# First layer: the low parts of the input weights made on GpSimd instead of VectorE

## The chip, the cores and the metric

One program on one core of a Trainium2 chip. The time is device microseconds of one execution. The kernel before took 3749.44 us as the median of three runs (3739.95 to 3749.61).

## The reference, cut to what matters

Two layers are applied to a prompt of 2048 frames and to 32 sample frames, all in float32. The first layer, the only one whose code changes, is

```
h = rms_norm(x, g) * (1 + scale) + shift            # 2048 x 1024
q, k, v, z = split(h @ w_in, 4)                     # w_in is 1024 x 4096
q, k = rms_norm(q), rms_norm(k)                     # per head of 64, 16 heads
o = attend(q, k, v, bias by clipped distance, chunks of 64, a band of 8 earlier chunks)
x = x + gate * (o * silu(z)) @ w_out
```

The second layer is latent attention with the same frame around it.

## The kernel before, in words

Every float32 matrix product is made of three TensorE products: each operand is held as a high part (rounded to the matmul's format) and a low part (the operand minus its high part). `mm3` (line 187, its products are lines 189, 190 and 191) adds high by high, high by low and low by high into one PSUM bank.

The first layer runs through 32 steps (the list `steps`): two halves of the prompt, in each half eight groups of two heads, and for each group two blocks of 512 frames. A step does the attention of its group and block (`prep`, `scores`, `values`, `finish`), and beside it, piece by piece by a plan of fractions of the step, the projection of the next step (`project` for q, k and v, `project_z` for z). So a group's weights are used for two steps, and a pair of steps takes about 83 us in the first half.

The weights of the next group are brought while the second block of the current group is projected. `fetch_w` loads a chunk of 256 rows (two k tiles) into one of two raw buffers `wr`; `split_w` then writes, for each k tile, the high part on ScalarE (line 458) and the low part on VectorE (line 459) into one of eight `wq` tiles of 128x384. Right after the split the raw buffer is loaded again. `fetch_z` and `split_z` (lines 470 and 471) do the same for z, 128x512 in one instruction, two tiles `wz` for each group. That is eight `wq` and two `wz` low parts for each pair of steps, 16 times in the kernel: once at the start, before anything is projected, and 15 times inside the steps.

Before the attention of a step can begin, q and k get their norm: line 511 copies the projection to `raw`, line 514 squares it, line 515 sums on VectorE, `rstd` (lines 174 to 184) makes 1/sqrt in small steps on VectorE and ScalarE, and line 520 multiplies: head 0 on VectorE, head 1 on GpSimd. TensorE then transposes `raw` (line 591). GpSimd also adds up the exponentials for the softmax sums (line 678, into `acc`), makes low parts of v (line 600), and in the second half low parts for the condition vectors' projection (line 149).

Each engine works through its queue in order. The order inside a queue is not the program's: a planner of the build places the instructions by the cost that it expects, so an instruction may stand far from its neighbours in the code. The DMAs all go through the queue of SyncE, in order too.

Of the kernel before, what the change touches and what calls it, by code (L numbers as in the profile page):

```python
# [11 lines left out]
ALU = mybir.AluOpType  # L12
# [19 lines left out]
def f32(ap):  # L32
    return ap if ap.dtype == F32 else ap.bitcast(F32)
# [66 lines left out]
def trunk(ctx: ExitStack, tc: tile.TileContext, I, O, stop=99):  # L100
    nc = tc.nc
    V, S, G, T = nc.vector, nc.scalar, nc.gpsimd, nc.tensor
# [268 lines left out]
    def at1(shape, name, dt=F32, bufs=1):  # L371
        return at.tile(shape, dt, tag=name, name=name, bufs=bufs)
# [79 lines left out]
    def split_w(g, c):  # L452
        raw = raws.pop((g, c))
        for i in range(2):
            w = at1([128, 2, 384], "wq", F32R, 8)
            hi, lo = (w[:, a, :].rearrange("p (h s d) -> p s h d", h=2, s=3) for a in range(2))
            src = raw[:, 384 * i:384 * i + 384].rearrange("p (s h d) -> p s h d", s=3, h=2)
            S.copy(hi, src)
            V.tensor_tensor(lo, src, f32(hi), ALU.subtract)
            Wg[g, 2 * c + i] = w  # L460

    def fetch_z(g, c):
# [4 lines left out]
    def split_z(g, c):  # L467
        raw = raws.pop((g, "z", c))[:, 0:512].rearrange("p (i c) -> p i c", i=4)
        w = at1([128, 4, 2, 128], "wz", F32R, 2)
        S.copy(w[:, :, 0, :], raw)  # L470
        V.tensor_tensor(w[:, :, 1, :], raw, f32(w[:, :, 0, :]), ALU.subtract)
        for i in range(4):
            Wz[g, 4 * c + i] = w[:, i]

# [16 lines left out]
    def project(s):  # L491
# [5 lines left out]
        for j in range(4):  # L497
            js = slice(128 * j, 128 * j + 128)
            p = bank("mm")[:, 0:384]
            for k in range(KT):  # L500
                w = Wg[g, k]
                mm3(p, (hT[:, k, 0, js], hT[:, k, 1, js]), (w[:, 0, :], w[:, 1, :]), k == 0, k == KT - 1)
                if k % 4 == 3 and blk % 2 and s["next_g"] is not None:
                    if j == 1:
                        fetch_w(s["next_g"], k // 4)
                    elif j == 3:
                        split_w(s["next_g"], k // 4)
                        fetch_w(s["next_g"], k // 4 + 2)
                if k in (2, 5):
                    yield  # L510
            S.copy(raw[:, j, :], p)
            qk = raw[:, j, :].rearrange("p (h c) -> p h c", h=2)[:, :, 0:128]
            sq = at1([128, 4, 128], "hs").rearrange("p j t -> p (j t)")[:, 0:256]
            S.activation(sq.rearrange("p (h c) -> p h c", h=2), qk, AF.Square)
            V.tensor_reduce(s16[:, 4 * j:4 * j + 4], sq.rearrange("p (h d) -> p h d", d=64), AX.X, ALU.add)
            if j == 3:
                r = rstd(s16, 16, 1.0 / 64).rearrange("p (j h e) -> p j h e", j=4, h=2)
                for h in range(2):
                    x = raw[:, :, 192 * h:192 * h + 128].rearrange("p j (e d) -> p j e d", d=64)
                    (V, G)[h].tensor_tensor(x, x, r[:, :, h, :].unsqueeze(3).broadcast_to([128, 4, 2, 64]), ALU.mult)  # L520
            yield
# [10 lines left out]
    def project_z(s):  # L532

        g, blk = s["g"], s["blk"]
        hT = HT[blk % 2]
        p = bank("mm")
        for k in range(KT):
            z = Wz[g, k]
            mm3(p, (z[:, 0, :], z[:, 1, :]), (hT[:, k, 0, :], hT[:, k, 1, :]), k == 0, k == KT - 1)
            if k % 2:  # L540
                if k == KT - 1:
                    s["z"] = at1([128, 512], "z", bufs=2)
                    S.copy(s["z"], p)
                if blk % 2 and s["next_g"] is not None:
                    c = (k - 3) // 2
                    if k in (3, 5):
                        split_w(s["next_g"], c + 2)
                        fetch_z(s["next_g"], c)
                    elif k == 7:
                        split_z(s["next_g"], 0)  # L550
                if k == KT - 1 and blk == 0:
                    sample_rows(lambda k, n: Wz[g, k][:, n, :], 128, 3, g)
                yield
        if blk % 2 and s["next_g"] is not None:
            split_z(s["next_g"], 1)
# [184 lines left out]
    for c in range(4):  # L740
        fetch_w(0, c)
        split_w(0, c)
# [28 lines left out]
    for c in range(2):  # L771
        split_z(0, c)
# [1223 lines left out]
```

## Time and profile before

| | |
|---|---|
| median of three runs | 3749.44 us |
| profiled execution, its own time | 3754.29 us |
| its span, first to last instruction | 3752.5 us |
| TensorE busy | 3511.9 us, 94% |
| VectorE busy | 2914.7 us, 78% |
| ScalarE busy | 2173.0 us, 58% |
| GpSimd busy | 1681.1 us, 45% |
| DMA | 412.91 MB, mean 110 GB/s |

The first layer's steps lie between about 130 and 1540 us of the span; the weights of the first group are split at 44 to 58 us. In the profile's names PE is TensorE's matmuls, PEld its weight loads, DVE VectorE, ACT ScalarE, POOL GpSimd, SP SyncE. "Idle before" is the time in which an engine stood still ahead of an instruction, and the arrow says what ended it. Busy shares are means over stages with different limits, so the change is read in the stretches where the splits stand.

### The profile page before, as it was taken

The page shows a single profiled execution, that of the slowest core. Times are in us where ns is not written, and L with a number is a line of the kernel's source. Part 1 is how long each engine was busy: PE and PEld are TensorE (multiplying, and loading weights), DVE is VectorE, ACT ScalarE, POOL GpSimd, SP SyncE. Part 2 cuts the span into 40 slices and gives each one's busy share as a digit, 9 for nine tenths or more (in the row PEclk, how much of TensorE's full clock was granted, in tenths as well). Part 3 has the DMA queues.
Part 4 walks back from the last instruction along what each step waited for, and adds up shares of the span by engine and source line. Part 5 has one row for each costly group of instructions (what it writes and reads, how often), then busy time and mean ns, then how long its engine had stood idle before and what let it go on. Part 6 is the DMA issues. An engine that isn't in the chain of part 4 may idle for free. (4 is left out here: it accounts for less than half of the span.)

```text
span 3752.5 us, 57503 instructions
## 1 busy us (share of the span) xinstructions
PE 3511.9 (94%) x17834; PEld 2871.1 (77%) x17834; DVE 2914.7 (78%) x6716; ACT 2173.0 (58%) x5302; POOL 1681.1 (45%) x1744
## 2 busy tenths in 40 slices
PE   7899999989999999899989999888999999998999
PEld 4778877867777777677878888767777787777887
DVE  4788888888888888776776766788888888885653
ACT  3556555676666666542223655556776677775542
POOL 0122222344544444340012444458888888884032
PEclk9899999999999999699999999979999999999999
DMA  5222222222333333363444666563233233223253
GB/s 175 69 60 59 69 62 75 81 76 82 99 96 92 96 92 96 96 190 126 132 152 149 181 203 185 171 186 90 74 84 98 67 93 92 68 77 111 89 189 118
DMA packets 441984, 412.91 MB, mean 110 GB/s; under 512 B 68820, under 2 KB 364296, under 8 KB 434636
## 3 DMA queue, kind: packets, MB, share of 16 engines
q1 hardware_dynamic: 441676, 409.23, 37.3%
q8 instruction: 141, 2.31, 0.3%
q14 instruction: 167, 1.37, 0.1%
HBM read 251.72 MB, written 140.10 MB: 104 GB/s over the span
## 5 line engine op out<-in xcount | busy, mean ns | idle before, releaser
L1544 DVE TENSOR_REDUCE mp@325_17580<-bank 128x1 f32<-128x512 f32 (+3 forms) x384 | 233.8, 615 | 28.3 <-PE bank L1543 26.3
L675 ACT ACTIVATE bank<-bank 128x512 f32<-128x512 f32 x448 | 200.3, 447 | 0.0
L678 POOL TENSOR_TENSOR acc@61_865<-acc@61_865,P@63_893 128x256 f32<-128x256 f32 (+3 forms) x64 | 52.9, 826 | 172.4 <-ACT P@63_893 L673 143.3
L1544 DVE TENSOR_REDUCE mp@326_17581<-bank 128x1 f32<-128x512 f32 (+1 forms) x192 | 116.9, 613 | 16.7 <-PE bank L1543 16.0
L1577 ACT ACTIVATE P@436_22812<-bank 128x512 f32<-128x512 f32 (+2 forms) x156 | 83.3, 534 | 74.3 <-issue 38.6
L1577 ACT ACTIVATE P@438_22814<-bank 128x512 f32<-128x512 f32 (+2 forms) x156 | 83.2, 534 | 67.3 <-issue 35.7
L718 DVE RECIPROCAL ez@69_1265<-ez@69_1265 128x128 f32<-128x128 f32 x128 | 117.6, 926 | 0.0
L1577 ACT ACTIVATE P@437_22813<-bank 128x512 f32<-128x512 f32 (+2 forms) x156 | 83.5, 535 | 55.3 <-PE bank L1570 11.3
L1577 ACT ACTIVATE P@435_22811<-bank 128x512 f32<-128x512 f32 (+2 forms) x156 | 83.4, 535 | 54.3 <-issue 13.0
L678 POOL TENSOR_TENSOR acc@61_865<-acc@61_865,P@64_894 128x256 f32<-128x256 f32 (+3 forms) x64 | 53.2, 831 | 114.9 <-ACT P@64_894 L673 92.4
L678 POOL TENSOR_TENSOR acc@62_866<-acc@62_866,P@65_895 128x256 f32<-128x256 f32 (+3 forms) x64 | 53.9, 841 | 106.3 <-ACT P@65_895 L673 103.0
L678 POOL TENSOR_TENSOR acc@62_866<-acc@62_866,P@63_893 128x128 f32<-128x128 f32 (+3 forms) x64 | 54.1, 846 | 103.1 <-ACT P@63_893 L673 96.0
L673 ACT ACTIVATE P@64_894<-bank 128x256 f32<-128x256 f32 (+3 forms) x128 | 52.3, 409 | 76.9 <-DVE bank L667 42.1
L678 POOL TENSOR_TENSOR acc@61_865<-acc@61_865,P@65_895 128x128 f32<-128x128 f32 (+3 forms) x64 | 53.6, 838 | 95.3 <-ACT P@65_895 L673 77.5
L673 ACT ACTIVATE P@63_893<-bank 128x384 f32<-128x384 f32 (+3 forms) x128 | 52.6, 411 | 75.1 <-DVE bank L667 42.7
L673 ACT ACTIVATE P@65_895<-bank 128x128 f32<-128x128 f32 (+3 forms) x128 | 52.4, 409 | 75.0 <-DVE bank L667 44.3
L678 POOL TENSOR_TENSOR acc@62_866<-acc@62_866,P@64_894 128x256 f32<-128x256 f32 (+3 forms) x64 | 54.4, 850 | 86.9 <-ACT P@64_894 L673 84.9
L149 POOL TENSOR_TENSOR ozl@175_14851<-ozl_@180_14859,ozh@173_14849 128x1024 fp32r<-128x1024 f32 x8 | 19.3, 2412 | 151.0 <-ACT ozh@173_14849 L148 151.0
L676 DVE TENSOR_TENSOR Pl@58_862<-bank,Ph@55_859 128x512 fp32r<-128x512 f32 (+3 forms) x150 | 71.3, 475 | 18.1 <-ACT bank L675 16.4
L676 DVE TENSOR_TENSOR Pl@60_864<-bank,Ph@57_861 128x384 fp32r<-128x384 f32 (+3 forms) x149 | 71.7, 481 | 11.6 <-ACT bank L675 9.3
L676 DVE TENSOR_TENSOR Pl@59_863<-bank,Ph@56_860 128x384 fp32r<-128x384 f32 (+3 forms) x149 | 72.7, 488 | 8.3 <-ACT bank L675 5.8
L1594 DVE TENSOR_TENSOR bank<-bank,P@437_22813 128x512 f32<-128x512 f32 (+2 forms) x108 | 66.5, 616 | 12.8 <-ACT P@437_22813 L1577 12.0
(2154 smaller groups left out, 14849.6 us busy)
## 6 DMA issues: line engine op xcount, KB each, us to landing
h<-hT@203_14883 SPq DMA_DIRECT2D x16, 1024.0 KB
N<-hl@389_17976 SPq DMA_DIRECT2D x32, 512.0 KB
N<-hl@390_17977 SPq DMA_DIRECT2D x32, 512.0 KB
wr@10_296<-in_a_w_in SPq DMA_DIRECT2D x64, 192.0 KB
wr@11_297<-in_a_w_in SPq DMA_DIRECT2D x64, 192.0 KB
xr@9_231<-in_ada_w SPq DMA_DIRECT2D x32, 256.0 KB
xr@8_230<-in_ada_w SPq DMA_DIRECT2D x32, 256.0 KB
h1@220_14902<-h SPq DMA_DIRECT2D x8, 1024.0 KB
```

Source lines behind the costliest of these rows:

```text
L149: (eng or V).tensor_tensor(twin(nc, raw), raw, f32(hi), ALU.subtract)
L673: S.activation(P[:, 0:w], st[:, 0:w], AF.Exp)
L675: S.activation(st[:, 0:w], st[:, 0:w], AF.Exp)
L676: V.tensor_tensor(Pl[:, 0:w], st[:, 0:w], f32(Ph[:, 0:w]), ALU.subtract)
L678: G.tensor_tensor(u["acc"][:, qs], u["acc"][:, qs], P[:, 0:w], ALU.add)
L718: V.reciprocal(ez[:, cs], ez[:, cs])
L1544: V.tensor_reduce(mp[:, j, c:c + 1] if blk else m4[:, j:j + 1], X[:, 0:w], AX.X, ALU.max)
L1577: S.activation(P[:, 0:w], st[:, 0:w], AF.Exp)
L1594: V.tensor_tensor((u["acc"] if last else u["sum"])[:, qs], old, P[:, 0:w], ALU.add)
```

## The change

Both low parts, of `wq` and of `wz`, are subtracted by GpSimd. The high parts stay on ScalarE; the loads, buffers and program order stay as they are.

```
@@ split_w
             S.copy(hi, src)
-            V.tensor_tensor(lo, src, f32(hi), ALU.subtract)
+            G.tensor_tensor(lo, src, f32(hi), ALU.subtract)
             Wg[g, 2 * c + i] = w
@@ split_z
         S.copy(w[:, :, 0, :], raw)
-        V.tensor_tensor(w[:, :, 1, :], raw, f32(w[:, :, 0, :]), ALU.subtract)
+        G.tensor_tensor(w[:, :, 1, :], raw, f32(w[:, :, 0, :]), ALU.subtract)
```

## Rows read from the trace of the kernel before

**Rows 1.** Windows: busy us and (count) of each engine, TensorE's clock, DMA share, GB/s.
```profile
130.00:1440.00 1310.00, 1241.51 (x6450) 1016.62 (x6449) 1108.52 (x2895) 837.84 (x2104) 493.60 (x521) 0.99 0.28 80
```
**Rows 2.** Windows around the 15 splits: the third, the fourth last, the sum.
```profile
297.00:327.00 30.00, 27.16 (x141) 22.43 (x139) 26.46 (x61) 16.01 (x40) 5.92 (x7) 1.00 0.39 115
...
1203.00:1235.00 32.00, 30.38 (x143) 24.64 (x142) 26.99 (x63) 18.54 (x48) 11.91 (x13) 0.89 0.41 116
...
sum 438.00, PE 401.24 PEld 323.42 DVE 389.62 ACT 252.79 POOL 139.61; mean PE 26.75 PEld 21.56 DVE 25.98 ACT 16.85 POOL 9.31
```
**Rows 3.** Waits of TensorE, 130 to 1440 us: total us, times, longest.
```profile
PE bank L591 <- DVE raw@23_443 L520: 13.0, 15, 1.7
PE bank L659 <- DVE Pl@59_863 L676: 12.0, 18, 2.2
PE bank L659 <- DVE Pl@60_864 L676: 8.4, 17, 0.7
...
PE bank L190 <- DVE wq@16_304 L459: 2.1, 1, 2.1
```
**Rows 4.** Groups of instructions on VectorE, 44 to 1440 us: the moved instructions.
```profile
L459 DVE TENSOR_TENSOR wq@19_307<-wr@11_297,wq@19_307 128x384 fp32r<-128x384 f32 x16 | 12.4, 777 | 0.1
L471 DVE TENSOR_TENSOR wz@42_606<-wr@10_296,wz@42_606 128x512 fp32r<-128x512 f32 x16 | 12.0, 748 | 0.1
L471 DVE TENSOR_TENSOR wz@43_607<-wr@11_297,wz@43_607 128x512 fp32r<-128x512 f32 x16 | 10.9, 681 | 1.5 <-ACT wz@43_607 L470 1.4
...
L459 DVE TENSOR_TENSOR wq@16_304<-wr@10_296,wq@16_304 128x384 fp32r<-128x384 f32 x16 | 8.7, 547 | 0.0
```
**Rows 5.** Groups of instructions on GpSimd by shape, 100 to 800 us.
```profile
L436 POOL TENSOR_TENSOR HT0@0_124<-hs@20_334,HT0@0_124 128x512 fp32r<-128x512 f32 x8 | 10.7, 1335 | 27.8 <-DVE HT0@0_124 L435 27.8
...
L678 POOL TENSOR_TENSOR acc@62_866<-acc@62_866,P@65_895 128x384 f32<-128x384 f32 x9 | 10.5, 1166 | 10.2 <-ACT P@65_895 L673 7.1 <-ACT Ph@55_859 L674 2.9
...
L678 POOL TENSOR_TENSOR acc@61_865<-acc@61_865,P@64_894 128x384 f32<-128x384 f32 x8 | 8.1, 1014 | 13.5 <-ACT P@64_894 L673 13.5
```
**Rows 6.** Order on VectorE in a split window: start us, us, engine, instruction.
```profile
303.10 0.16 DVE L174 TENSOR_SCALAR ms<-s 128x16 f32<-128x16 f32 x1
...
305.64 0.17 DVE L183 SCALAR_TENSOR_TENSOR rt<-rt,ms 128x16 f32<-128x16 f32 x1
305.73 0.55 DVE L459 TENSOR_TENSOR wq@16_304<-wr@10_296,wq@16_304 128x384 fp32r<-128x384 f32 x1
306.19 0.17 DVE L184 SCALAR_TENSOR_TENSOR rs<-rt,rs 128x16 f32<-128x16 f32 x1
306.28 0.55 DVE L459 TENSOR_TENSOR wq@17_305<-wr@10_296,wq@17_305 128x384 fp32r<-128x384 f32 x1
306.75 1.54 DVE L520 TENSOR_TENSOR raw@23_443<-raw@23_443,rs 128x512 f32<-128x512 f32 x1
```
**Rows 7.** Order on GpSimd in the same window.
```profile
298.48 0.46 POOL L678 TENSOR_TENSOR acc@61_865<-acc@61_865,P@63_893 128x128 f32<-128x128 f32 x1 [7.23 <-ACT P@63_893 L673]
306.50 1.24 POOL L520 TENSOR_TENSOR raw@23_443<-raw@23_443,rs 128x512 f32<-128x512 f32 x1 [7.56 <-DVE rs L184]
```
**Rows 8.** A late window: VectorE's line 183 and the GpSimd instruction beside it.
```profile
1311.75 1.20 DVE L183 SCALAR_TENSOR_TENSOR rt<-rt,ms 128x16 f32<-128x16 f32 x1
...
1311.63 1.28 POOL L678 TENSOR_TENSOR acc@62_866<-acc@62_866,P@64_894 128x512 f32<-128x512 f32 x1 [4.51 <-ACT P@64_894 L673]
```
**Rows 9.** Durations of single lines, 130 to 1440 us: min/median/max ns, first and last start.
```profile
L183 DVE SCALAR_TENSOR_TENSOR rt<-rt,ms x37: 141/165/1202, 144.5 to 1407.1; 128x16 f32<-128x16 f32 x29, 128x1 f32<-128x1 f32 x8
L520 DVE TENSOR_TENSOR raw@23_443<-raw@23_443,rs x15: 682/1535/1693, 145.7 to 1408.4; 128x512 f32<-128x512 f32 x15
```
**Rows 10.** Order around the one wait for a split; ACT, then DVE, then PE.
```profile
834.48 0.51 ACT L458 CAST wq@16_304<-wr@10_296 128x384 fp32r<-128x384 f32 x1 [1.11 <-DMA wr@10_296<-in_a_w_in]
...
836.99 0.55 DVE L459 TENSOR_TENSOR wq@16_304<-wr@10_296,wq@16_304 128x384 fp32r<-128x384 f32 x1
837.59 0.44 PE L190 MATMUL bank<-wq@16_304,HT0@0_124 128*128 128x384 f32 x1 [2.10 <-DVE wq@16_304 L459]
```
**Rows 11.** Window of ten us after that wait, columns as in rows 1.
```profile
835.00:845.00 10.00, 6.54 (x23) 4.41 (x23) 9.69 (x19) 8.05 (x18) 4.00 (x3) 0.83 0.45 122
```
**Rows 12.** One high part on ScalarE behind its load, and its low part later on VectorE.
```profile
302.65 0.51 ACT L458 CAST wq@18_306<-wr@11_297 128x384 fp32r<-128x384 f32 x1 [0.18 <-DMA wr@11_297<-in_a_w_in]
...
313.69 0.56 DVE L459 TENSOR_TENSOR wq@18_306<-wr@11_297,wq@18_306 128x384 fp32r<-128x384 f32 x1
```
**Rows 13.** The start: first low part, last `wq` low part, first matmul, on their engines.
```profile
44.41 0.56 DVE L459 TENSOR_TENSOR wq@12_300<-wr@10_296,wq@12_300 128x384 fp32r<-128x384 f32 x1
...
51.28 0.56 DVE L459 TENSOR_TENSOR wq@19_307<-wr@11_297,wq@19_307 128x384 fp32r<-128x384 f32 x1
...
48.29 0.44 PE L189 MATMUL bank<-wq@12_300,HT0@0_124 128*128 128x384 f32 x1 [0.30 <-DVE HT0@0_124 L435]
```

More of the change, by code (lines that the diff above doesn't have):

```diff
@@ L458, in split_w @@
             S.copy(hi, src)
-            V.tensor_tensor(lo, src, f32(hi), ALU.subtract)
+            G.tensor_tensor(lo, src, f32(hi), ALU.subtract)
             Wg[g, 2 * c + i] = w
@@ L470, in split_z @@
         S.copy(w[:, :, 0, :], raw)
-        V.tensor_tensor(w[:, :, 1, :], raw, f32(w[:, :, 0, :]), ALU.subtract)
+        G.tensor_tensor(w[:, :, 1, :], raw, f32(w[:, :, 0, :]), ALU.subtract)
         for i in range(4):
```

## The prediction

> **What bounds the kernel now.** I read the busy windows of the first layer's steps first, then TensorE's waits there, then the order on VectorE and GpSimd around one split.
>
> The windows say that TensorE is the bound of this stage and VectorE is next: in 1310 us TensorE is busy 1241.5 us, VectorE 1108.5 us (85%), GpSimd 493.6 us (38%), at a granted clock of 0.99 [rows 1]. TensorE stands idle 1310 - 1241.5 = 68.5 us. The same view cut to the 15 stretches around a split (438 us) has TensorE busy 401.2 us, so 36.8 us idle, 8.4%; the other 872 us hold 31.7 us, 3.6%. In those stretches VectorE is busy 389.6 of 438 us, 89%, and GpSimd only 139.6 us, 32% [rows 1, 2]. So more than half of the idle time lies in a third of the stage, where VectorE is fullest and the moved work stands. That is the most the change can touch: 36.8 us if every wait there went, and 36.8 - 0.036 x 438 = 21 us if these stretches became like the others.
>
> The waits say which step ends late. The longest entry is the transposition of `raw` (line 591) waiting for VectorE's normalising multiplication (line 520): 13.0 us in 15 waits, 0.87 us for each pair of steps [rows 3]. The next two are score matmuls behind the low part of the probabilities (20.4 us together, over the whole stage). One single wait, 2.1 us, is for a weight split itself.
>
> The order on VectorE shows why line 520 is late. Its small steps 183 and 184 and itself are in one chain, and two weight splits stand in between: wq 16 starts at 305.73 and lets line 184 start at 306.19, wq 17 starts at 306.28 and lets line 520 start at 306.75, so 0.46 + 0.47 = 0.93 us on the chain [rows 6]. Line 520 then takes 1.54 us although the least it takes is 0.68: GpSimd began its own half at 306.50 and held it up [rows 6, 7, 9].
>
> **The change part by part.** *Removed from VectorE:* 128 low parts of 128x384 and 32 of 128x512. The ten groups (eight of `wq` from 8.7 to 12.4 us, two of `wz`, 12.0 and 10.9) add up to about 97 us of busy time [rows 4]; instructions overlap at their ends, so a `wq` split occupies its queue for about 0.47 us [rows 6]. Per pair of steps that is 8 x 0.47 + 2 x 0.6 = 5 us of VectorE's 83.
>
> *Added to GpSimd:* the trace has no such split on GpSimd. Nearest are its additions of the same shape, 1.01 us undisturbed and 1.17 us where VectorE disturbs them, and for 128x512 the low part of h, 1.34 us [rows 5]. I take 1.05 us for `wq` and 1.35 us for `wz`: 128 x 1.05 + 32 x 1.35 = 178 us in all, 11.1 us for each pair. Bounds are 128 x 1.01 + 32 x 1.34 = 172 us, and, with the disturbed price and 1.34 raised in the same ratio to 1.55, 128 x 1.17 + 32 x 1.55 = 199 us. The Trainium skill's GPSIMD Engine Reference (4.1 Engine selection) calls GpSimd about two times slower for two-input elementwise work; by that, 0.55 us would become 1.1 us, 0.68 us 1.36 us, and the sum 184 us, an estimate that the durations of rows 5 bear out.
>
> GpSimd has room for it: it is busy 32% of the split windows and would be at (139.6 + 15 x 11.1) / 438 = 70%. In the window shown it does one small addition between 291 and 306 us [rows 7]. What stands behind the added instructions in its queue is the other half of line 520, whose transposition comes much later, and the additions of line 678, which hand back three P buffers to ScalarE.
>
> *Gain, the chain into line 591.* The 0.93 us leave the chain in every pair, against an average wait of 0.87 us. If nothing came instead, the whole 13.0 us would go. Bounds: 0 and -13.
>
> *Gain, the one wait for a split.* At 837 us TensorE waits 2.1 us for wq 16. ScalarE ended the high part at 834.99; GpSimd would end the low part at 834.99 + 1.05 = 836.04 instead of 837.54, so 1.5 us earlier [rows 10]. After that wait the granted clock is 0.83 for ten us [rows 11], which is another 1.7 us of lost matmul time. Together about -3; bounds 0 and -3.8.
>
> *Loss, contention.* In the late windows line 183 takes 1.20 us instead of 0.165: it starts at 1311.75 while GpSimd works from 1311.63 to 1312.91, and ends just after it [rows 8, 9]. Line 520 shows the same, a median of 1.535 against a least of 0.682 [rows 9]. So VectorE instructions with two operands in SBUF wait for the end of the GpSimd instruction that began first. The change raises GpSimd's share in the split windows by 38 points. The chain has five VectorE steps that can meet it (174, 182, 183, 184, 520), each with a chance 0.38 greater and a mean wait of half a GpSimd instruction, 0.5 us: 5 x 0.38 x 0.5 = 0.95 us a pair, 14 us over 15 pairs. I count half of it, 8 us rather than 14, because the steps 182 and 183 wait for ScalarE anyway and because a split that no longer stands between 184 and 520 lets VectorE's half of 520 start first more often. Bounds 0 and +14.
>
> The Trainium skill says of this in Perfetto Trace Analysis (Optimizing Scalar/DVE Operations) that the two engines share a read port, and that moving work between them might not help. By that rule the gains above would be returned in full; the trace agrees that such blocking happens here, and my half is a choice against the rule's full weight. It is the fourth case below.
>
> *Added wait, the reload of `wr`.* The raw buffer is free when the low part has been made, so a slower split delays the next load. ScalarE's high part of wq 18 now waits 0.18 us for its load, and stands ahead of exponentials and of line 180 in ScalarE's queue [rows 12]. Four splits of 1.05 in place of 0.47 us end up to 2.3 us later if they queue up on GpSimd; the high parts come about 0.5 us apart. If the planner keeps the order, ScalarE waits up to about 1 us more per pair. On the other hand wq 18's low part now lies on VectorE until 313.69, 10.5 us after its high part [rows 12]; on GpSimd it can follow at once, and the z load behind it starts earlier. I put the two at nothing, bounds -3 and +10.
>
> *The start.* Here GpSimd is free and VectorE full: eight splits begin between 44.41 and 51.28, and the first matmul starts at 48.29 [rows 13]. VectorE saves about 0.6 us ahead of that matmul, and the later reloads may cost as much. Nothing, bounds -1 and +2.
>
> *The sum:* -13 - 3 + 8 = -8 us. The profiled execution took 3754.29 us, its span 3752.5; -8 makes 3746.3. It lies 4.85 us over the median of the runs, so the forecast for the median is 3749.44 - 8 = 3741 us. Its own range is 3730 to 3750.
>
> A measurement of this kernel can tell about 0.3%, 11 us, from no change; faster means under 3738, slower over 3761.
>
> **The rivals.**
> *The windows become like the others.* All that VectorE did late in the split windows moves forward, and the score matmuls behind the low probabilities gain too: -21 us (worked out above), and about 4 us of clock with it (one window has a clock of 0.89 [rows 2]): 3724 us. For it: VectorE's 89% there. Against it: much of the chain waits for ScalarE or TensorE, and the moved work comes back as contention.
>
> *The chain gets slower.* The small steps of the norm run back to back, and GpSimd with a row of splits in its queue takes the turn after each of them. Then each of the five steps waits not by chance but nearly always for 0.5 us: 5 x 0.5 = 2.5 us a pair, minus the 0.93 saved, so +1.6 us in each of 15 pairs, +24 us: 3773 us. TensorE waits for this chain already [rows 3], so all of it counts. It decides from the point where more than about two of the five steps are blocked in each pair. For it: line 183's 1.20 us. Against it: its median is 0.165 us, blocking is rare today.
>
> *It does not do what it says.* VectorE's splits were put off until TensorE needed them (wq 18) and so filled gaps only, or the shared port returns all: nothing changes, 3749 us. Against it: wq 16 and 17 stand inside the chain.
>
> **How the numbers follow.** Forecast 0.38, windows like the others 0.30, slower chain 0.22, nothing 0.10. The forecast's own spread puts 0.10 of its 0.38 under 3738, the second case 0.27 of its 0.30, so faster 0.37. Slower than 3761 is 0.20 of the third case's 0.22. The rest, 0.43, is no change. The range reaches to both outer cases, 3720 to 3768, in the third case down from its 3773 as far as its 0.22 needs.
>
> **What would show it.** Right: in the 15 windows VectorE's busy time falls by about 5 us each and GpSimd's rises by about 11; line 591's wait for line 520 falls from 13.0 us to under 6; the wait for wq 16 is under 1 us. GpSimd's `wq` split takes 1.0 to 1.2 us. Wrong: lines 174 to 184 with medians over 0.5 us, or line 591 waiting over 20 us, means the slower chain; ScalarE waiting for `wr` by over 15 us in all would mean the reload; TensorE's idle time in the windows under 20 us is the faster rival. A planner that orders the queues anew would move waits to lines that are not named here.

## The result and the profile after

The changed kernel takes 3800.33 us as the median of four runs (3796.58 to 3801.61) against 3746.73 us before (now also of four runs; the three ahead of the prediction gave 3749.44): a ratio of 1.0144, 95% interval 1.0126 to 1.0162. It is slower by 54 us; 3741 us was forecast, and the range ended at 3768.

The profiled executions differ by 42.3 us (3796.58 against 3754.29; before lies 7.6 us over its median, the changed one 3.8 under). The end of VectorE's line 520 in each step serves as a mark of progress. The second one comes at 147.1 us before and 150.5 after, so 3.5 us are lost at the start; the last one at 1505.6 and 1551.0. So 42 us are lost between them, and 3 us come back in the second layer. The windows between these marks, of before and then of after (span, busy us and count of PE, PEld, DVE, ACT and POOL, granted clock, DMA share, GB/s):

```profile
147.00:1506.00 1359.00, 1286.26 (x6671) 1052.19 (x6672) 1153.18 (x3013) 864.93 (x2171) 518.52 (x544) 0.99 0.29 81
```
```profile
150.00:1551.00 1401.00, 1303.33 (x6665) 1085.22 (x6664) 1107.13 (x2867) 862.31 (x2171) 667.39 (x689) 0.96 0.28 78
```

TensorE's idle time goes from 1359 - 1286.3 = 72.7 us to 97.7, +25 us. Its busy time rises by 17 us for the same matmuls, while the granted clock falls from 0.99 to 0.96. VectorE is relieved by 46 us, GpSimd loaded with 149. The change also made the planner order the queues anew: taken as sequences of instructions (operation, tiles, shapes), TensorE's queues of before and after agree by about half only. So a new order is a rival for the loss, besides the moved work itself.

TensorE's waits after, 130 to 1440 us, which answer to [rows 3] (total us, times, longest):

```profile
PE bank L591 <- DVE raw@23_443 L520: 17.7, 10, 2.6
PE bank L659 <- DVE Pl@59_863 L676: 15.7, 12, 3.7
PE bank L659 <- DVE Pl@60_864 L676: 9.8, 14, 2.2
PE bank L591 <- DVE raw@22_442 L520: 7.5, 5, 2.2
...
PE bank L659 <- DVE Pl@58_862 L676: 6.7, 6, 2.5
```

Line 591 waits 25.2 us for line 520, fewer times but for longer. The wait for a split, 2.1 us in [rows 3], is gone.

Where the time goes is seen in the window of [rows 6, 7], some 12 us later now (start us, us, engine, instruction; VectorE, then GpSimd, then TensorE):

```profile
309.75 1.49 DVE L699 TENSOR_TENSOR pair@68_1092<-acc@61_865 64x512 f32<-64x512 f32 x1 [1.60 <-POOL acc@61_865 L678]
...
313.34 0.78 DVE L174 TENSOR_SCALAR ms<-s 128x16 f32<-128x16 f32 x1
...
316.59 0.11 DVE L183 SCALAR_TENSOR_TENSOR rt<-rt,ms 128x16 f32<-128x16 f32 x1
...
317.22 0.72 DVE L184 SCALAR_TENSOR_TENSOR rs<-rt,rs 128x16 f32<-128x16 f32 x1
317.86 0.42 DVE L663 TENSOR_TENSOR bank<-bank,BT1@40_597 128x256 f32<-128x256 f32 x1
318.19 1.42 DVE L520 TENSOR_TENSOR raw@23_443<-raw@23_443,rs 128x512 f32<-128x512 f32 x1
...
309.25 0.47 POOL L678 TENSOR_TENSOR acc@61_865<-acc@61_865,P@63_893 128x128 f32<-128x128 f32 x1
309.67 1.03 POOL L459 TENSOR_TENSOR wq@15_303<-wr@11_297,wq@15_303 128x384 fp32r<-128x384 f32 x1
...
313.07 1.02 POOL L459 TENSOR_TENSOR wq@18_306<-wr@11_297,wq@18_306 128x384 fp32r<-128x384 f32 x1
...
316.60 1.31 POOL L471 TENSOR_TENSOR wz@42_606<-wr@10_296,wz@42_606 128x512 fp32r<-128x512 f32 x1 [1.54 <-ACT wz@42_606 L470]
318.01 1.05 POOL L520 TENSOR_TENSOR raw@23_443<-raw@23_443,rs 128x512 f32<-128x512 f32 x1
...
319.66 0.66 PE L591 MATMUL bank<-ident,raw@23_443 128*128 128x128 f32 x4 [2.21 <-DVE raw@23_443 L520]
...
322.65 0.52 PE L190 MATMUL bank<-wq@12_300,HT0@0_124 128*128 128x384 f32 x1
322.98 0.52 PE L191 MATMUL bank<-wq@12_300,HT0@0_124 128*128 128x384 f32 x1
```

Line 174 lasts until GpSimd's wq 18 ends at 314.09, and line 184 until wz 42 ends at 317.91: 0.78 and 0.72 us in place of 0.16 and 0.17 [rows 6]. Line 520 lasts 1.42 us because GpSimd's half began first, as before. TensorE stands 2.21 us, and 0.96 us once more at 321.7, for a low part of the probabilities. Then 128x384 matmuls start 0.33 us apart. The clock of this window before the stall and of ten us after it:

```profile
300.00:320.00 20.00, 17.19 (x88) 14.58 (x87) 15.48 (x33) 12.00 (x29) 12.39 (x13) 1.00 0.33 92
322.00:332.00 10.00, 10.00 (x39) 8.53 (x39) 6.65 (x17) 3.45 (x9) 2.92 (x4) 0.70 0.50 147
```

1.00 is 2.4 GHz; 0.70 is a mean over a stretch of which a part ran at 1.2 GHz. So the stall is paid twice.

The small steps of the norm over the first layer (130 to 1560 us), before and after (busy us, mean ns | idle before):

```profile
L183 DVE SCALAR_TENSOR_TENSOR rt<-rt,ms 128x16 f32<-128x16 f32 (+2 forms) x40 | 10.0, 254 | 0.1
L174 DVE TENSOR_SCALAR ms<-s 128x16 f32<-128x16 f32 (+1 forms) x39 | 7.2, 188 | 0.1
L184 DVE SCALAR_TENSOR_TENSOR rs<-rt,rs 128x16 f32<-128x16 f32 (+2 forms) x40 | 6.3, 161 | 0.1
L182 DVE TENSOR_TENSOR rt<-rs 128x16 f32<-128x16 f32 (+2 forms) x40 | 5.9, 152 | 3.2 <-ACT rs L181 3.0
```
```profile
L184 DVE SCALAR_TENSOR_TENSOR rs<-rt,rs 128x16 f32<-128x16 f32 (+2 forms) x40 | 15.3, 382 | 0.2
L174 DVE TENSOR_SCALAR ms<-s 128x16 f32<-128x16 f32 (+1 forms) x39 | 14.6, 376 | 0.1
L182 DVE TENSOR_TENSOR rt<-rs 128x16 f32<-128x16 f32 (+2 forms) x40 | 11.7, 291 | 1.0 <-ACT rs L181 0.3
L183 DVE SCALAR_TENSOR_TENSOR rt<-rt,ms 128x16 f32<-128x16 f32 (+2 forms) x40 | 10.9, 271 | 0.1
```

They sum to 29.4 us before and 52.5 after: +23 us on the chain into line 591, 16 of them within the 15 us ahead of an even-numbered mark, where the splits stand.

The 3.5 us of the start are in part of the same kind. The first matmul on `wq` 12 comes at 50.24 in place of 48.29 [rows 13]; it waits for line 435 on VectorE, and the steps ahead of that were held up by splits:

```profile
45.36 0.94 DVE L182 TENSOR_TENSOR rt<-rs 128x1 f32<-128x1 f32 x1
46.34 0.93 DVE L183 SCALAR_TENSOR_TENSOR rt<-rt,ms 128x1 f32<-128x1 f32 x1
...
44.84 1.45 POOL L459 TENSOR_TENSOR wq@13_301<-wr@10_296,wq@13_301 128x384 fp32r<-128x384 f32 x1
46.25 1.00 POOL L459 TENSOR_TENSOR wq@14_302<-wr@11_297,wq@14_302 128x384 fp32r<-128x384 f32 x1
```

Each of the two lasts until the split beside it ends (46.29 and 47.25); both take 0.15 us at this place before. The planner also put lines 485 to 488 ahead of line 435 here. The split itself cost what was forecast; the cheapest and the dearest groups on GpSimd, after, 130 to 1440 us:

```profile
L471 POOL TENSOR_TENSOR wz@43_607<-wr@11_297,wz@43_607 128x512 fp32r<-128x512 f32 x14 | 20.8, 1487 | 2.7 <-ACT wz@43_607 L470 2.7
...
L459 POOL TENSOR_TENSOR wq@12_300<-wr@10_296,wq@12_300 128x384 fp32r<-128x384 f32 x14 | 14.2, 1015 | 44.9 <-ACT wq@12_300 L458 44.9
```

### The profile page after: what moved, and what is told of

Its sections match the earlier page's. It is cut to its first block, busy times and chain, and to the rows that moved or that the text cites. A ratio compares the mean times of both kernels' runs of the same rounds, so it can differ in the third digit from the quotient of the medians.

```text
span 3794.8 us, 57608 instructions
## 1 busy us (share of the span) xinstructions
PE 3530.0 (93%) x17834; PEld 2905.8 (77%) x17834; DVE 2872.7 (76%) x6556; ACT 2169.4 (57%) x5302; POOL 1844.3 (49%) x1904
## 5 line engine op out<-in xcount | busy, mean ns | idle before, releaser
L1544 DVE TENSOR_REDUCE mp@326_17581<-bank 128x1 f32<-128x512 f32 (+1 forms) x192 | 117.2, 614 | 16.8 <-PE bank L1543 16.3
L673 ACT ACTIVATE P@64_894<-bank 128x256 f32<-128x256 f32 (+3 forms) x128 | 52.5, 410 | 64.6 <-DVE bank L667 35.1
L676 DVE TENSOR_TENSOR Pl@59_863<-bank,Ph@56_860 128x384 fp32r<-128x384 f32 (+3 forms) x149 | 72.7, 488 | 15.8 <-ACT bank L675 14.4
```

The lines of the kernel that those rows point to most:

```text
L673: S.activation(P[:, 0:w], st[:, 0:w], AF.Exp)
L676: V.tensor_tensor(Pl[:, 0:w], st[:, 0:w], f32(Ph[:, 0:w]), ALU.subtract)
L1544: V.tensor_reduce(mp[:, j, c:c + 1] if blk else m4[:, j:j + 1], X[:, 0:w], AX.X, ALU.max)
```

## The experiments

Three theories of the loss. P: GpSimd's subtractions read SBUF and hold up VectorE's steps. Q: what queues behind the splits on GpSimd comes late. R: a slower split frees the raw buffer late, and its next load holds up ScalarE. Ratios are to the kernel before on the same chip, with 95% intervals.

**Halves of the change.** e3_late_only leaves the first four `wq` low parts of a group on VectorE, e4_early_only leaves all the others there, e1_wz_only all `wq`.

```
e3  (G if c > 1 else V).tensor_tensor(lo, src, f32(hi), ALU.subtract)
e4  (G if c < 2 else V).tensor_tensor(lo, ...)    # and V for wz
e1  V.tensor_tensor(lo, ...)                      # G for wz
```

> Only the last four of a group's eight wq low parts and the two wz ones on GpSimd; the first four stay on VectorE. Theory Q (queue): in the changed kernel a short addition into acc (0.47 us) stands behind the first three splits on GpSimd, VectorE's line 699 waits 1.6 us for it in order, and with it the norm chain up to line 520; TensorE's wait at line 591 grows from 0.6 to 2.2 us and its clock then falls. Without the first four on GpSimd that wait is gone: within 12 us of the kernel before, line 591 under 1 us in the first half. Theory P (port): the steps 174 to 184 and 520 are blocked by GpSimd instructions that read SBUF; the last four splits run just beside them, so most of the loss stays: 30 to 50 us slower than before.

> Only the first four of a group's eight wq low parts on GpSimd; the other four and wz stay on VectorE. Theory Q: the addition into acc still stands behind them, so most of the loss is there: 30 to 55 us slower than before, line 699 idle about 1.6 us a pair. Theory P: these splits are over before the steps 174 to 184 run, so 0 to 15 us slower.

> Only the two wz low parts of each group on GpSimd, the eight wq low parts on VectorE as before. Theory R: the wz loads are the last of a group and the next group's first load comes a step later, so little is held up: ratio 1.000 to 1.004. Theory P: 2 of 10 low parts, 24% of the added GpSimd time, most of it beside the chain: about a quarter of the loss, ratio 1.002 to 1.005.

Measured 1.0072 [1.0049, 1.0094], 1.0064 [1.0044, 1.0083] and 1.0040 [1.0026, 1.0053]. e3, 30 us slower, lies at the lower edge of P's range; e4, 25 us slower, misses both ranges (0 to 15 and 30 to 55); e1 lies in both. Over the whole kernel the halves add up (0.72 + 0.64 against 1.44%), so it is not one unlucky instruction. In the first prompt half (up to the 15th mark) they don't: the early splits cost nothing (-0.5 us), the late ones 12.0, all together 24.6. The early ones cost in the second.

**One wait behind the splits.** Line 699 above waits 1.6 us for an addition that stands between two splits. e5_last_add_V puts the last such addition on VectorE.

```
- G.tensor_tensor(u["acc"][:, qs], u["acc"][:, qs], P[:, 0:w], ALU.add)
+ last = h == 0 and blk % 2 == 0 and n == (3 if blk == 0 else 7)
+ (V if last else G).tensor_tensor(...)
```

> All low parts on GpSimd as in the changed kernel, but the last addition into acc of head 0 in the steps whose neighbour is split beside them (16 instructions of 128x128) is made on VectorE, so that it stands behind no split. Theory Q: at most half of the loss is left, up to 25 us slower than before. Theory P: as slow as the changed kernel, 45 to 60 us slower than before.

1.0129 [1.0100, 1.0158]: this wait does not carry the loss, although line 591 waits 19.8 us for line 520 in place of 25.2.

**Memsets in place of the subtraction.** In the next runs GpSimd writes zeros, so the low parts of the first layer's input weights are left out (in e15_read_free further down too). e7_memset has two memsets for each subtraction.

> GpSimd writes zeros twice into each low part in place of the subtraction: it leaves out the low parts of the first layer's input weights, reads nothing from SBUF, and wr is free as soon as ScalarE has read it. Theory P: what blocks is reading beside reading, so the loss is gone, within 12 us of before or faster. Theory Q: as far as the two memsets last as long as a split (about 1 us), the addition into acc still waits behind them and 25 to 50 us stay; if they last under half of that, both theories expect no loss and the run tells nothing.

1.0011 [0.9993, 1.0028]: without the subtraction the loss is gone. But memsets also don't wait for ScalarE, and hold no raw buffer. So the next runs tie them. The cuts are shortened and show `wq`; for `wz` e13 has one and a half memsets and e14 two whole ones.

```
e12  tiny(); memset(lo); memset(lo); tiny()      # tiny: the subtraction on 128x2
e13  tiny(); memset(lo); tiny()                  # holds the raw buffer
e14  tiny(); memset(lo); memset(lo[:, 128:384])  # frees it at once
```

> Each of GpSimd's 160 subtractions is replaced by four instructions on the same tile: a 128x2 subtraction, two memsets of the whole low part, the 128x2 subtraction again. So GpSimd's work still waits for ScalarE's high part, still holds the raw buffer until it ends, and takes at least as long (2 x 0.42 us and two small ones, against 1.02 us), but reads next to nothing of SBUF. The low parts of the first layer's input weights are left out. Theory P (GpSimd's reads hold up VectorE's two-operand steps): the loss goes, ratio to before 1.005 or less, line 591 waits under 16 us. Theory Q (what queues behind GpSimd's splits, the acc additions and the reload of wr, comes late): the loss stays, 3790 to 3805, ratio 1.010 to 1.015.

> Each GpSimd subtraction replaced by a 128x2 subtraction, one memset of the low part (for wz one and a half), and the 128x2 subtraction again: GpSimd occupied for about 1.0 us for each wq and 1.3 for each wz as in the changed kernel, the raw buffer held as long, next to no reads. The low parts of the first layer's input weights are left out. Theory P (the reads block VectorE): loss mostly gone, ratio 1.005 or less. Theory R (the raw buffer comes free late, so its next load comes late and ScalarE, which works in order, stands at a high part with the norm's Ln and the exponentials behind it): the loss stays, ratio 1.009 to 1.015, and ScalarE waits for loads of wr by 25 us or more (before 21.5, changed kernel 27.1, previous run with memsets between two small subtractions 44.7).

> As the previous one without the second 128x2 subtraction and with a longer memset in its place: GpSimd is occupied as long and still waits for ScalarE's high part, but the raw buffer comes free after the first 0.2 us. The low parts of the first layer's input weights are left out. Theory R: the loss goes, ratio 1.004 or less, ScalarE waits for wr by under 20 us. Theory Q (the acc additions and the multiplication of line 520 queue behind the splits): the loss stays, ratio 1.009 to 1.015. Theory P: as for the previous one, so 1.005 or less for both.

e12 1.0127 [1.0099, 1.0155], e13 1.0092 [1.0066, 1.0118], e14 0.9990 [0.9976, 1.0004]. This went against P as the only cause: two kernels without the reads are slow (e12 also keeps GpSimd for longer, 222 us between the 2nd and the 15th mark against 212). It seemed to speak for R, until the four raw buffers below. e13 waits elsewhere than the changed kernel: 16.3 us for the load of `QG`, where the changed kernel waits 3.6. e14 also answers the planner's new order: its queue on TensorE agrees with the changed kernel's by 89% and with before's by under half, and it loses nothing.

**Reads without the hold, the missing cell.**

```
e15  tiny(); G.tensor_tensor(lo, f32(hi), f32(hi), ALU.subtract)
```

> Each GpSimd subtraction replaced by a 128x2 subtraction (which lets go of the raw buffer) and a full subtraction of the high part from itself: two full reads of SBUF as in the changed kernel and 0.2 us more GpSimd time for each, but the raw buffer is free after 0.2 us. The low parts of the first layer's input weights are left out (they are zero). Theory R (only the late release of the raw buffer costs): as without reads, ratio 0.997 to 1.003. Theory P (the reads block VectorE's two-operand steps, and the hold costs apart from it): the part of the loss that the hold leaves over, ratio 1.004 to 1.010; VectorE's steps 174 and 182 to 184 are again held up as in the changed kernel (mean of line 184 over 0.3 us).

1.0134 [1.0113, 1.0155]: the whole loss, more than either theory said. This pair is the cleanest comparison here. Between the second and the last mark the queues of e14 and e15 agree by over 99% on TensorE, ScalarE and VectorE, so the planner's order on these three is out of the question. GpSimd's instructions differ by the edit itself; what that does to one addition in its queue is counted below. Windows between the same marks, e14 and e15:

```profile
147.00:1514.00 1367.00, 1292.24 (x6671) 1073.38 (x6671) 1082.34 (x2869) 860.37 (x2174) 637.14 (x980) 0.97 0.29 81
```
```profile
149.00:1553.00 1404.00, 1310.07 (x6664) 1083.06 (x6665) 1095.46 (x2867) 862.05 (x2169) 664.58 (x832) 0.96 0.28 78
```

Of 37 us, 19 are idle time of TensorE and 18 more busy time for the same matmuls, much as between before and after. The same place in both, e14 first (the transposition is line 597 in e14 and 593 in e15; the multiplication 526 and 522; 725 and 721 are the changed kernel's 719):

```profile
315.71 0.16 DVE L184 SCALAR_TENSOR_TENSOR rs<-rt,rs 128x16 f32<-128x16 f32 x1
315.79 0.68 DVE L725 TENSOR_TENSOR z@54_855<-z@54_855,ez@69_1305 128x512 f32<-128x512 f32 x1
316.39 0.68 DVE L526 TENSOR_TENSOR raw@23_459<-raw@23_459,rs 128x512 f32<-128x512 f32 x1
...
315.48 0.53 POOL L476 MEMSET wz@42_622<- 128x512 f32 x1
316.07 0.53 POOL L477 MEMSET wz@42_622<- 128x512 f32 x1
316.56 1.42 POOL L526 TENSOR_TENSOR raw@23_459<-raw@23_459,rs 128x512 f32<-128x512 f32 x1
...
317.13 0.66 PE L597 MATMUL bank<-ident,raw@23_459 128*128 128x128 f32 x4
```
```profile
323.82 0.97 DVE L184 SCALAR_TENSOR_TENSOR rs<-rt,rs 128x16 f32<-128x16 f32 x1
324.72 0.68 DVE L721 TENSOR_TENSOR z@54_845<-z@54_845,ez@69_1285 128x512 f32<-128x512 f32 x1
325.32 1.53 DVE L522 TENSOR_TENSOR raw@23_451<-raw@23_451,rs 128x512 f32<-128x512 f32 x1
...
323.72 1.04 POOL L473 TENSOR_TENSOR wz@42_614<-wz@42_614 128x512 fp32r<-128x512 f32 x1
324.87 1.43 POOL L522 TENSOR_TENSOR raw@23_451<-raw@23_451,rs 128x512 f32<-128x512 f32 x1
...
326.91 0.66 PE L593 MATMUL bank<-ident,raw@23_451 128*128 128x128 f32 x4 [2.21 <-DVE raw@23_451 L522]
```

Beside a memset line 184 takes 0.16 us. Beside the reading subtraction it takes 0.97, until that ends. That also turns the order at the multiplication: GpSimd's half begins first, and VectorE's takes 1.53 us in place of 0.68. TensorE, which did not wait at all, waits 2.21 us. From the fourth mark to the 15th, each of the six intervals from an even-numbered to an odd-numbered step has such a stall in e15 (1.5 to 2.3 us) and none of over 0.7 us in e14. In this stretch TensorE's idle time rises from 20.1 to 32.0 us, and its wait for `raw@23` from 0.2 to 11.8: that is the whole rise.

Not all of a stall is blocking. VectorE's 939 instructions stand in the same order there, so they can be compared one by one. Against e14, each of the six stalls has 0.85 us from the blocked multiplication, 0.7 to 0.85 from line 184 (in five of the six), and 0.97 from a wait of theory Q: line 701 (705 in e14) waits for an addition into `acc` that stands behind three whole splits in e15, and ahead of the third one's memsets in e14, first e14, then e15:

```profile
308.20 0.46 POOL L684 TENSOR_TENSOR acc@61_885<-acc@61_885,P@63_913 128x128 f32<-128x128 f32 x1
```
```profile
315.95 0.83 POOL L460 TENSOR_TENSOR wq@14_302<-wq@14_302 128x384 fp32r<-128x384 f32 x1
316.74 0.46 POOL L680 TENSOR_TENSOR acc@61_875<-acc@61_875,P@63_903 128x128 f32<-128x128 f32 x1
```

So about 1.6 of 2.6 us by which the multiplication ends later are blocking, and 1.0 is what queues behind the splits. The splits follow each other at nearly the same pace on GpSimd in both runs (about 1.0 us and 1.06).

The Trainium skill, SBUF — State Buffer, section Who interferes with whom, says that a VectorE instruction with two SBUF inputs contends with a GpSimd instruction that reads SBUF, not with one that only writes it, and it calls the ports that the two share an exclusive lock. The fences agree for line 184, which lasts until the subtraction ends (324.79 and 324.76); lines 182 to 184 take 24.3 us in all in e14 and 36.1 in e15 (130 to 1560 us).

**Freeing the chain.** e8_psum keeps one operand of each small step in PSUM; e10_before_psum is its control.

```
ms, yp, u = (ps[:, 16 * i:16 * i + 16] for i in range(3))   # PSUM
V.tensor_scalar(ms, ssq, inv, EPS, ALU.mult, ALU.add)
...
V.tensor_tensor(t, yp, y, ALU.mult)
V.scalar_tensor_tensor(u, t, -0.5, ms, ALU.mult, ALU.mult)
V.scalar_tensor_tensor(y, u, 1.5, y, ALU.add, ALU.mult)
```

> The changed kernel, with the norm's chain (lines 174 to 184) rewritten for project alone so that each VectorE step of it has one operand in PSUM (the unused columns 384 to 447 of the last projection's bank) and at most one in SBUF; ScalarE writes 1/sqrt twice, one small activation more in each step of the first layer. Theory P: these steps are no longer held up (their means fall to 0.2 us or less from up to 0.4), most of the loss goes, ratio 1.000 to 1.007; line 520 still has two SBUF operands and keeps its share. Theory Q: the loss stays, ratio 1.011 to 1.016, plus up to 32 x 0.2 = 6 us for the activation.

> The kernel before, with the norm's chain of project rewritten as in the run e8_psum, so that its VectorE steps have one operand in PSUM: the control of that run. The additional activation costs up to 0.2 us in each of 32 steps, 6 us. If the rewriting itself costs nothing: 1.000 to 1.002, and the e8_psum run's 1.0126 then is the changed split's loss with a chain that can't be blocked (theory P falls as the whole cause). If the rewriting costs much (1.005 or more), the e8_psum run's loss is mostly its own and theory P stands.

1.0126 [1.0106, 1.0147], control 0.9992 [0.9982, 1.0002]. Here I expected too much of P. The chain is free (line 591's counterpart waits 7.2 us for `raw@23`, 8.8 in the control), but the steps behind it are held up instead. In e8, line 735 is the changed kernel's 719, 615 its 599, 692 its 676 and 675 its 659:

```profile
320.81 1.53 DVE L735 TENSOR_TENSOR z@54_835<-z@54_835,ez@69_1265 128x512 f32<-128x512 f32 x1
322.27 1.08 DVE L615 CAST VT01@33_573<-raw@23_443 128x256 fp32r<-128x256 f32 x1
323.27 0.55 DVE L692 TENSOR_TENSOR Pl@60_864<-bank,Ph@57_861 128x384 fp32r<-128x384 f32 x1
...
323.87 0.33 PE L675 MATMUL bank<-QA@45_613,KA10@26_566 128*128 128x128 f32 x1 [1.57 <-DVE Pl@60_864 L692]
```

1.53 and 1.08 us stand where 0.68 (line 725 of e14 above) and 0.28 (line 615's median in the control) would do: TensorE's 1.57 us have moved to the low part behind them. That wait is 17.4 us in all against 10.0 in the control. What runs beside the two steps on GpSimd is no split but its half of the multiplication (320.30 to 321.80) and an addition into `acc` (321.76 to 323.20), both behind the splits in its queue.

**Smaller pieces.** e11_pieces makes each `wq` low part in three instructions of 128x128.

> The changed kernel with each wq low part made by GpSimd in three instructions of 128x128 (q, k and v parts) in place of one of 128x384. Theory P: a VectorE step that meets one is held up by 0.4 us at most in place of 1.0, so the loss shrinks to a half or less, ratio 1.003 to 1.009, although GpSimd works a little longer. Theory Q: GpSimd's work and what queues behind it are the same or longer, ratio 1.013 to 1.020.

1.0217 [1.0192, 1.0243], a miss of both theories: GpSimd is busy for 229 us between the 2nd and the 15th mark against 212 in the changed kernel, and line 591's counterpart waits 26.7 us for `raw@23`.

**Work on GpSimd, no relief.** e6_both lets VectorE make each low part and GpSimd make it again.

> VectorE makes each low part as in the kernel before and GpSimd makes it again in place: GpSimd's new work without VectorE's relief, and the raw buffer held until the second has ended. If VectorE's relief is worth what the prediction said (16 us), this is slower than the changed kernel by about that: 3810 to 3825, ratio 1.016 to 1.020. If the relief is worth nothing, as the memset run suggests, and the GpSimd side is the whole loss: 3795 to 3808, ratio 1.012 to 1.015. A line 591 that waits over 25 us speaks for theory P.

1.0235 [1.0218, 1.0253]. That is above both ranges. It adds an own wait (TensorE waits 12 us for GpSimd's low parts), so it doesn't price the relief. e14 comes nearer, with 71 us less VectorE work than before in the windows shown and 0.9990, but GpSimd is still occupied there; no run has the work simply gone.

**More raw buffers.** In the first half the buffers for rows of `x` lie idle; groups 1 to 7 take them as third and fourth raw buffer. e18_wr4_psum adds the PSUM chain.

```
+ more = c > 1 and 2 <= groups[0] <= 8
+ raw = raws[g, c] = xraw()[:, 0:768] if more else at1([128, 768], "wr", bufs=2)
```

> The changed kernel with four raw buffers in place of two for the groups 1 to 7 of the first half (the third and fourth are the buffers for rows of x, which are idle there). No load then waits for a split of its own group. Theory R: the loss of the first half (24.6 us up to the 15th norm, 18.5 of it after the third) goes down to under 10 us, ratio 1.007 to 1.010, since the second half keeps two buffers. Theory P: the loss stays, 1.012 to 1.016.

> The control: the kernel before with the same four raw buffers. Both theories: no difference, 0.997 to 1.002; under theory R it may gain up to 5 us in the first half, since ScalarE's waits for raw loads (21.5 us in all) shrink there.

> The changed kernel with both the four raw buffers and the norm's chain with one operand in PSUM. Theory R and P together: the first half's loss is gone, under 5 us at the 15th norm, ratio 1.004 to 1.008. If neither is the cause: 1.012 or more.

1.0150 [1.0130, 1.0170], control 0.9979 [0.9968, 0.9991], both cures 1.0124 [1.0106, 1.0142]. With four buffers ScalarE's waits for `wr` in the changed kernel fall from 26 to 11 us, and at the 15th mark it is still 33 us late, not under 10. R is not its cause.

**Longer memsets, and the best version.**

> As e14_free with three full memsets behind the 128x2 subtraction (for wz too), so GpSimd is occupied for about 1.4 us for each wq and 1.7 for each wz, a third longer than in the changed kernel, without the reads and without holding the raw buffer. The low parts of the first layer's input weights are left out. Theory P (the reads): no loss, ratio 0.997 to 1.005. Theory Q (GpSimd's time, and what queues behind it there): more than the changed kernel's loss, ratio 1.015 to 1.025.

> The kernel before, low parts on VectorE, with the four raw buffers of e17_before_wr4 (0.9979) and the norm's chain with one operand in PSUM of e10_before_psum (0.9992). If the two gains add up: 0.995 to 0.999, 3735 to 3750 us, below both kernels. If they are the same waits: 0.998, as e17_before_wr4.

e19 1.0181 [1.0160, 1.0203]: GpSimd's time may cost as much without the reads, so Q is not excluded as a way to lose. But e19's queue on TensorE agrees with e14's by only 84%, and its largest wait is another one:

```profile
PE bank L629 <- DMA QG@46_644<-QA@44_642: 23.2, 8, 3.9
```

e20, low parts on VectorE, is 0.9945 [0.9925, 0.9965]: clearly faster than both kernels, and a little below the range that I gave. It keeps the low parts where they were.

## Why the prediction was wrong

*The loss by contention* is the step that failed. Its mechanism was right, down to the lines named; its size was not. "I count half of it, 8 us rather than 14": measured are +23 us on lines 174 to 184 alone, 16 of them just ahead of the marks with splits, over the upper bound of 14, which was the mean estimate itself and no worst case. Of the reasons for halving, ScalarE's cover held for line 183 (+0.9 us) but not for 182 (+5.8), and line 520 does not start first more often in a way that counts: 37.6 us before, 37.0 after. A mean chance of 0.38 for each step was too little. GpSimd's row of splits lies where the chain lies, and a blocked step can meet the next split too. And the term left out a second part: what stands behind the splits in GpSimd's queue comes late. I had named the additions of line 678 there and gave them no term (0.97 us of each stall in e15).

*The clock* was missing in the loss. I put it into a gain (the wait at 837 us [rows 10, 11]) and the faster rival, but not behind the stalls that the change might add: 17 of 42 us are more busy time, at 0.96 in place of 0.99.

*The gain of 13 us in line 591* did not come. Even without contention (e14) that line waits 11.2 us (6.1 for `raw@23`, 5.1 for `raw@22`), and the matmuls behind the low probabilities then wait longer: 31.1 us for all three `Pl` buffers, against 22.7 before. VectorE's share of 89% was read as a bound, but 71 us less work there bought nothing measurable in e14. *The wait for wq 16* did go (2.1 us).

*GpSimd's prices* were right: 1.02 to 1.25 us for `wq` (mean 1.08), 1.30 and 1.49 for `wz`. *The reload* was rightly left at nothing: ScalarE's waits for `wr` rise from 20.6 to 26.1 us (130 to 1440 us), and shorter waits with more buffers don't help; the sign that I gave (over 15 us) was met before the change already. *The start* cost 3.5 us, over its bound of +2: GpSimd is free there, but its splits block VectorE's steps ahead of line 435, which the term for contention left out, and the planner moved four more steps ahead of it.

The rival *the chain gets slower* is nearest to what happened, at 54 us in place of 24. Its sign "line 591 waiting over 20 us" showed (25.2). The other, medians over 0.5 us, did not: they stay at 0.16 to 0.17 us, and only the means rise (line 184: 161 to 382 ns). The trace had shown blocking in the worst cases of [rows 8, 9], and a median cannot see it.

What stays open: why e13, which reads next to nothing, is 36 us late at the 15th mark. From the 2nd mark on GpSimd is busy for 195 us there, against 199 in e14; the clock is 0.93, and TensorE's order is another. e12 and e19 lose without full reads too; they keep GpSimd longer than the changed kernel. So the blocking by reads is shown in the trace of the first half, where it makes up about 1.6 of 2.6 us of each stall; how the second half's loss divides was not worked out, and reads are not the only way in which this stage loses 1%.

## What to carry to other kernels

Before work goes to another engine, list the instructions on the critical chain that share something with that engine, and lay the moved instructions beside them in time; a mean chance is too kind where both come in bursts. A busy share near 90% is no bound by itself: run a kernel in which that work is simply gone (not done here), and move it only if that one is faster. Look also at what stands behind the moved work in the new engine's queue. And price a new stall of the fullest engine with the clock that it loses afterwards.

## What the runs showed of the hardware

A VectorE instruction of 0.16 us on 128x16 took 0.97 us beside a GpSimd instruction that began 0.10 us earlier: its size does not protect it. Beside a memset the two-operand steps run free, but line 174, with one operand, does not: in e14 it starts at 312.72 and takes 0.42 us, until a memset that began at 312.69 ends. The blocking goes both ways: GpSimd's wq 16 takes 1.48 us beside VectorE's line 699 in the window above (starts 310.64), against 1.02.

A stall of 2.2 us of TensorE, with one of 0.96 us close behind it, was followed by ten us at a mean granted clock of 0.70 in the changed kernel; after the stall of 2.2 us in e15 it was 0.83 (327 to 337 us). In e14, where the stall is missing, the ten us after the transposition have 1.00.
